# Thirty-two tokens of the second layer by gathered rows, modulation rows moved and halved, and wider gate products, in a two-layer backbone

## The chip, the cores and the metric

The kernel is one program on one core of a Trainium2 chip. Its time is the device time of one execution, in microseconds (us). A core has TensorE (PE: matrix products; the profile lists its weight loads apart as PEld), VectorE (DVE), ScalarE (ACT), GpSimd (POOL), SyncE (SP) and 16 DMA engines that all queues share. Each engine works through its own instructions in the order of the program.

## The reference

Two layers run over 256 context and 256 latent tokens of width 1024. In each, a modulated norm feeds four token mixers, and a second modulated norm `h` feeds a product-key expert layer. The modulation is six vectors (shift, scale and gate, twice), a product of silu(c) with a weight matrix: c for latents, c_ctx for context. Cut to the expert layer:

```python
def block(xb):                                  # 128 tokens
    qry = (xb @ wq).reshape(128, 8, 2, 128)
    s = einsum('thpk,hpnk->thpn', qry, sub_keys)
    sv, si = top_k(s, 16)                        # 16 of 128, for 8 heads x 2 halves
    cand_s = sv[:, :, 0, :, None] + sv[:, :, 1, None, :]
    cand_i = si[:, :, 0, :, None] * 128 + si[:, :, 1, None, :]
    fs, fpos = top_k(cand_s, 16)                 # 16 of the 256 pairs
    eidx = take_along_axis(cand_i, fpos)         # 8 x 16 = 128 experts of 16384
    gate = softmax(fs)
    act = gelu(einsum('td,thkd->thk', xb, u[eidx]))
    return einsum('thk,thkd->td', gate * act, v[eidx])
```

The second layer needs no context output: there the expert layer takes the 256 latents alone, and of its six vectors only the first two are used for both kinds of token.

## The kernel before

Tokens lie along the columns; the width lies on partitions in 8 blocks of 128 (`KD`). Products of high precision are three matmuls (`mm3`, L72 to L74): high x high, high x low, low x high, with each weight split by ACT (the high part) and DVE (what is left).

`peer(l)` is the expert layer, dense for most tokens: all 16384 experts are computed for all tokens and masked by gates. It has these stages.

- **Query stage** (`norm2`, `query`): 8 chunks of `wq`, then scores against the keys, then `top16` on DVE. After each chunk comes one pair of u-blocks.
- **u stage** (`u_blocks`): 64 pairs of blocks of 128 experts. A block takes 24 matmuls (8 x `mm3`) with `wd` columns, a gelu, and a store of the activation to DRAM (`ad`). `u_prep` loads a pair into one of 2 `raw` buffers and splits it into tiles of the pool `spl` (10 tiles). `wd` is 384 in layer 0 and 256 in layer 1.
- **Routing** (`route`, one per 128 tokens) turns the top 16 of each half into 128 expert numbers and gates per token (`fin`), all on DVE. It finds a key's index by comparing a position with 0..15 (L1295), multiplying by the indices (L1297) and adding up.
- **Gates** (`gate_hot`, `gates`): one-hot matrices per token, multiplied on PE into a 128x128 gate matrix (tile `pg`), 8 tokens a group, 16 groups per 128 tokens; stored to DRAM (`gd`), or, for the first 40 blocks of layer 1 (`FOLD`), multiplied at once into `kept`.
- **v stage** (`v_blocks`): again 64 pairs. Load v, activations (`va`) and gates (`vg`), multiply them (L1474), split the product into `wh` and `wl` and v into two `spl` tiles, and add 24 matmuls a block into 8 accumulators `f`.

In layer 0 the first 128 tokens are "apart": `tokens_apart` fetches for each the 128 rows of u that it needs, one gather of 128 rows of 4 KB a step (indirect DMA, issued by POOL), and multiplies each with `ht`, the token's own row of `h` (`dot`, L1384); the same for v, added into `facc` (L1391). That is 256 gathers. `rows_to` deals them out: `PHASE1` = 168 of them along the u stage, into tiles of `spl`, and the other 88 along the v stage, into 4 tiles `row`. Layer 1 has none.

`ada_row` computes 128 numbers of a modulation vector on DVE: a weight row tile (512 KB) times silu(c), summed along the row (L305), once for c and once for c_ctx. 56 of them run in layer 0's v stage, one after each pair: 8 for layer 0's last gate and all 48 of layer 1. `pin` keeps an instruction in the place of the program; otherwise a scheduler of the language chooses each engine's order when the program is built.

Of the kernel before, what the change touches and what calls it, by code (L numbers as in the profile page):

```python
# [12 lines left out]
U32 = mybir.dt.uint32  # L13
# [23 lines left out]
APART = 128  # L37
ROWS = 4
PHASE1 = 168
# [14 lines left out]
class Kernel:  # L54
# [39 lines left out]
    def build(self):  # L94
        tc, nc, A = self.tc, self.nc, self.A
        with ExitStack() as es:
# [25 lines left out]
            self.wd = [TA - APART, TC]  # L122
# [172 lines left out]
    def ada_row(self, pool, l, n):  # L295

        nc = self.nc
        if l not in self.mod:
            self.mod[l] = self.cst.tile([128, 6, KD, 2], F32, name=f"mod{l}")
        s, k = divmod(n, KD)  # L300
        w = pool.tile([128, 1024], F32, name="adaw", bufs=2)
# [4 lines left out]
        nc.vector.tensor_add(self.mod[l][:, s, k], self.mod[l][:, s, k], self.badat[:, l, s, k:k + 1].to_broadcast([128, 2]))  # L306
# [727 lines left out]
    def peer(self, l):  # L1034
# [5 lines left out]
        apart = (w - wd) // 128  # L1040
        with ExitStack() as es:
# [19 lines left out]
            with ExitStack() as e1:  # L1061
# [4 lines left out]
                with ExitStack() as e2:  # L1066
# [14 lines left out]
                    with self.order("DVE", "Activation"):  # L1081
# [6 lines left out]
                        self.norm2(aff, ts, hh, hl, self.rs_mm(w, scr, self.psum.tile([128, 512], F32, name="mm")), ht=ht)  # L1088
                    for ch in range(8):
# [5 lines left out]
                        u_pair()  # L1095
                sp = None
                if apart:
                    self.far = ep1(tc.tile_pool(name=f"far{l}", bufs=1, reuse_waits="tile"))
                with ExitStack() as e2:
# [12 lines left out]
                    if apart:  # L1112
# [3 lines left out]
                        sp = self.tokens_apart(l, fin[0], ht)  # L1116
                        next(sp)
                    first = apart
# [7 lines left out]
                    def u_next():  # L1126
                        u_pair()
                        rows_to(PHASE1 * (used[0] - u0) // (64 - u0))
                    for n, _ in enumerate(routes[first]):
                        if n % RN[l] == 0:  # L1130
                            u_next()
                    nd = nt - first
                    cost = [GW if t + 1 < nd else 1.0 for t in range(nd) for _ in range(16)]
                    left = 64 - used[0] - GL[l]
                    done = 0
                    sl = self.gate_slots(fin[first])
                    hot = self.gate_hot(sl, 0)
# [3 lines left out]
                    for x in range(16 * nd):  # L1141
                        t, g = divmod(x, 16)
                        while done < int(left * sum(cost[:x + 1]) / sum(cost) + 1e-6):
# [3 lines left out]
                        if t + 1 < nd:  # L1147
                            next(routes[first + t + 1], None)
                            if g == 14:
                                for _ in routes[first + t + 1]:  # L1150
                                    pass
                                sl2 = self.gate_slots(fin[first + t + 1])
# [617 lines left out]
```

## Time and profile before

| | |
|---|---|
| median of 3 runs | 2875.59 us (2870.84 to 2876.46) |
| profiled execution, its own time | 2874.08 us |
| its span, first to last instruction | 2872.0 us |
| busy: PE, DVE, ACT, POOL | 94%, 76%, 44%, 14% of the span |
| DMA | 662.88 MB, mean 231 GB/s |

A busy PE is not a PE at its peak: its matmuls overlap, so what one costs in a stream is the distance from start to start, not its duration. From the times of the matmuls, the stages lie as follows (us from the start): mixers of layer 0 to 427; query stage to 595; routing of the tokens apart to 655; rest of the u stage to 1202; v stage to 1775; mixers of layer 1 to 2029; query stage to 2135; routing and first gates to 2250; u stage to 2492; v stage to 2860.

### The profile page before, as it was taken

The page shows a single profiled execution, that of the slowest core. Times are in us where ns is not written, and L with a number is a line of the kernel's source. Part 1 is how long each engine was busy: PE and PEld are TensorE (multiplying, and loading weights), DVE is VectorE, ACT ScalarE, POOL GpSimd, SP SyncE. Part 2 cuts the span into 40 slices and gives each one's busy share as a digit, 9 for nine tenths or more (in the row PEclk, how much of TensorE's full clock was granted, in tenths as well). Part 3 has the DMA queues.
Part 4 walks back from the last instruction along what each step waited for, and adds up shares of the span by engine and source line. Part 5 has one row for each costly group of instructions (what it writes and reads, how often), then busy time and mean ns, then how long its engine had stood idle before and what let it go on. Part 6 is the DMA issues. An engine that isn't in the chain of part 4 may idle for free.

```text
span 2872.0 us, 47065 instructions
## 1 busy us (share of the span) xinstructions
PE 2701.9 (94%) x18199; PEld 2491.3 (87%) x18199; DVE 2178.1 (76%) x4703; ACT 1265.1 (44%) x2185; POOL 389.9 (14%) x354
## 2 busy tenths in 40 slices
PE   8989989999999987999999998988999999999998
PEld 5766758998888877999999997766999999999998
DVE  5665667689999976799999986655789767666665
ACT  5564644343344432343333334654545445444443
POOL 0010000004444343322222310000000000000000
PEclk9999899999999998999999999999999999999999
DMA  7111423237899999999999984211535766877774
GB/s 265 71 48 45 162 88 134 90 136 280 309 369 367 358 364 343 337 341 374 370 370 368 368 301 136 89 37 52 194 136 187 250 240 234 292 240 248 249 246 143
DMA packets 268752, 662.88 MB, mean 231 GB/s; under 512 B 16496, under 2 KB 146672, under 8 KB 258928
## 3 DMA queue, kind: packets, MB, share of 16 engines
q1 hardware_dynamic: 198688, 450.04, 45.0%
q0 software_dynamic: 36864, 134.23, 12.6%
q10 hardware_dynamic: 32976, 75.61, 6.9%
q8 instruction: 142, 2.33, 0.3%
q14 instruction: 82, 0.67, 0.1%
HBM read 585.37 MB, written 74.45 MB: 230 GB/s over the span
## 4 chain that ended last, share of the span: by engine, by line
PE 70%; DVE 16%; DMA 5%; issue 4%; ACT 3%; SPq 1%; POOL 0%; ACTq 0%; DVEq 0%; POOLq 0%
PE pu L72 8%; PE pu L74 8%; PE pu L73 8%; PE f L73 8%; PE f L74 8%; PE f L72 7%; PE fp L72 3%; PE fp L73 3%; PE fp L74 3%; PE pg L1349 2%; DVE junk L305 2%; DVE spl L1469 2%; PE mm L72 2%; PE mm L73 2%; PE mm L74 2%
## 5 line engine op out<-in xcount | busy, mean ns | idle before, releaser
L72 PE MATMUL pu<-h2h,spl 128*128 128x384 f32 (+1 forms) x2048 | 649.6, 317 | 39.4 <-ACT spl L1417 38.3
L73 PE MATMUL f<-wl,spl 128*128 128x384 f32 (+1 forms) x2048 | 635.3, 310 | 11.0 <-DVE wl L1476 11.0
L74 PE MATMUL pu<-h2h,spl 128*128 128x384 f32 (+1 forms) x2048 | 636.9, 313 | 8.2 <-DVE spl L1418 7.9
L73 PE MATMUL pu<-h2l,spl 128*128 128x384 f32 (+1 forms) x2048 | 639.4, 312 | 0.0
L74 PE MATMUL f<-wh,spl 128*128 128x384 f32 (+1 forms) x2048 | 629.2, 309 | 0.0
L72 PE MATMUL f<-wh,spl 128*128 128x384 f32 (+1 forms) x2048 | 511.7, 311 | 11.6 <-ACT wh L1475 8.4
L1468 ACT CAST spl<-raw 128x1024 fp32r<-128x1024 f32 x256 | 268.0, 1050 | 389.8 <-PE f L73 343.0
L72 PEld LDWEIGHTS pu<-h2h,spl 128*128 128x128 f32 x2048 | 393.0, 192 | 47.3 <-ACT spl L1417 44.0
L1469 DVE TENSOR_TENSOR spl<-raw,spl 128x1024 fp32r<-128x1024 f32 x256 | 312.6, 1225 | 158.8 <-ACT spl L1468 157.5
L1417 ACT CAST spl<-raw 128x1024 fp32r<-128x1024 f32 x256 | 266.6, 1049 | 343.1 <-PE pu L73 229.4
L73 PEld LDWEIGHTS f<-wl,spl 128*128 128x128 f32 x2048 | 389.7, 190 | 16.8 <-DVE wl L1476 16.1
L74 PEld LDWEIGHTS pu<-h2h,spl 128*128 128x128 f32 x2048 | 391.7, 191 | 12.7 <-DVE spl L1418 12.4
L1418 DVE TENSOR_TENSOR spl<-raw,spl 128x1024 fp32r<-128x1024 f32 x256 | 311.8, 1221 | 110.9 <-ACT spl L1417 108.8
L73 PEld LDWEIGHTS pu<-h2l,spl 128*128 128x128 f32 x2048 | 393.1, 192 | 0.3
L72 PEld LDWEIGHTS f<-wh,spl 128*128 128x128 f32 x2048 | 377.9, 190 | 16.1 <-ACT wh L1475 11.3
L74 PEld LDWEIGHTS f<-wh,spl 128*128 128x128 f32 x2048 | 389.2, 190 | 0.0
L418 DVE TENSOR_TENSOR spl<-raw,spl 128x512 fp32r<-128x512 f32 (+1 forms) x226 | 150.3, 704 | 72.7 <-ACT spl L414 62.5
L1435 ACT ACTIVATE act<-pu 128x384 f32<-128x384 f32 (+1 forms) x216 | 95.7, 443 | 218.7 <-PE pu L74 213.6
L1378 POOL DMA_INDIRECT spl<-in_un,ix x92 | 128.8, 1400 | 387.5 <-DVE fp L1246 244.0
L347 POOL TENSOR_TENSOR ms<-ms,mhalf 128x4 f32<-128x4 f32 (+1 forms) x5 | 4.8, 953 | 1264.1 <-DVE sq L345 833.9
L1475 ACT CAST wh<-va 128x384 fp32r<-128x384 f32 (+1 forms) x216 | 100.0, 467 | 168.5 <-PE f L74 79.5
L414 ACT CAST spl<-raw 128x512 fp32r<-128x512 f32 (+1 forms) x226 | 130.5, 629 | 76.8 <-PE fp L73 28.9
(305 smaller groups left out, 4547.6 us busy)
## 6 DMA issues: line engine op xcount, KB each, us to landing
raw<-in_ut SPq DMA_DIRECT2D x128, 1024.0 KB
raw<-in_v SPq DMA_DIRECT2D x128, 1024.0 KB
adaw<-in_wadat SPq DMA_DIRECT2D x56, 512.0 KB
ad<-act ACTq DMA_DIRECT2D x64, 384.0 KB
gd<-gstage ACTq DMA_DIRECT2D x12, 2048.0 KB
vg<-gd SPq DMA_DIRECT2D x32, 768.0 KB
va<-ad SPq DMA_DIRECT2D x64, 384.0 KB
raw<-in_win SPq DMA_DIRECT2D x22, 1024.0 KB
```

What stands on the lines that cost most here:

```text
L72: mm(ps, ah, bh, start=first, stop=False, **kw)
L73: mm(ps, ah, bl, start=False, stop=False, **kw)
L74: mm(ps, al, bh, start=False, stop=last, **kw)
L414: return self.nc.scalar.copy(p[0][o], w[:, o])
L418: return eng.tensor_tensor(p[1][o], w[:, o], p[0][o].bitcast(F32), op=ALU.subtract)
L1378: nc.gpsimd.indirect_dma_start(r, None, tabs[which], bass.IndirectOffsetOnAxis(ix[:, s:s + 1], 0))
L1417: self.pin(nc.scalar.copy(uh, self.u[:, n % 2]), n < 3)
L1418: self.pin(nc.vector.tensor_tensor(ul, self.u[:, n % 2], uh.bitcast(F32), op=ALU.subtract), n < 3)
L1435: nc.scalar.activation(a[:, b, :w], ps[:, :w], AF.Gelu)
L1468: nc.scalar.copy(vh, v[:, b])
L1469: nc.vector.tensor_tensor(vl, v[:, b], vh.bitcast(F32), op=ALU.subtract)
L1475: nc.scalar.copy(wh[:, :w], a[:, b, :w])
```

## The change

1. Layer 1 sets 32 of its 256 tokens apart (`APART = (128, 32)`), so that its u and v matmuls have 224 columns and 4 of its 32 gate groups fall away. A token's 128 experts are spread over four partitions: partitions q*32 to q*32+31 hold the same 32 tokens with 32 experts each, so there are 32 gathers of u rows and 32 of v rows. `ht` and `fin` are copied to the four quarters by small DMAs on SP, and a matrix `fsel` adds the quarters up at the end.
2. `PHASE1` is (144, 26): layer 0 makes 144 of its 256 gathers in the u stage and 112 in the v stage; layer 1 makes 26 of 64 in its u stage.
3. Of layer 1's modulation rows, those of the last four vectors are multiplied with silu(c) alone, not c_ctx. 24 of them move into layer 0's query stage, 4 after each chunk from the second on, with weight tile, junk tile and silu(c) in `spl`. The other 32 run after every other pair of the v stage, from one buffer `adaw` instead of two.
4. `v_blocks` multiplies and splits the gated values of both blocks of a pair in one instruction each.
5. `route` keeps the indices (`sif`) twice side by side, so that the multiplication's second operand has an innermost run of two.

```diff
-APART = 128
+APART = (128, 32)
-PHASE1 = 168
+PHASE1 = (144, 26)
...
-            self.wd = [TA - APART, TC]
+            self.wd = [TA - APART[0], TC - APART[1]]
...
-    def ada_row(self, pool, l, n):
+    def ada_row(self, w, junk, csb, l, n, nv):
...
-        for j in range(2):
+        for j in range(nv):
             o = self.mod[l][:, s, k, j:j + 1]
-            self.pin(nc.vector.scalar_tensor_tensor(self.junk, w, 1.0, self.csb[:, j], op0=ALU.mult, op1=ALU.mult, accum_out=o))
+            self.pin(nc.vector.scalar_tensor_tensor(junk, w, 1.0, csb[:, j], op0=ALU.mult, op1=ALU.mult, accum_out=o))
...
+                        for q in range(apart, 128, apart):
+                            nc.sync.dma_start(ht[q:q + apart], ht[0:apart])
+                    extra = list(range(16, 40)) if l == 0 else []
...
                         u_pair()
+                        if extra and ch == 0:
+                            csb = self.ada_vector()
+                        for _ in range(min(4, len(extra)) if ch else 0):
+                            w1, junk = (self.spl.tile([128, 1024], F32, name="spl") for _ in range(2))
+                            self.ada_row(w1, junk, csb, 1, extra.pop(0), 1)
...
-                        extra = [(0, n) for n in range(40, 48)] + [(1, n) for n in range(48)]
+                        extra = [(0, n, 2) for n in range(40, 48)] + [(1, n, 2) for n in range(16)] + [(1, n, 1) for n in range(40, 48)]
...
-                        if extra:
-                            self.ada_row(self.vp, *extra.pop(0))
+                        if extra and n % 2 == 0:
+                            self.ada_row(self.vp.tile([128, 1024], F32, name="adaw", bufs=1), self.junk, self.csb, *extra.pop(0))
...
-        sif = rw.tile([128, 8, 2, 16], BF16, name="sif")
-        nc.vector.tensor_copy(sif, si)
+        sif = rw.tile([128, 2, 128, 2], BF16, name="sif")
+        for j in range(2):
+            nc.vector.tensor_copy(sif[:, j].rearrange("p (h n) b -> p h n b", h=8), si[:, :, j, :, None].to_broadcast([128, 8, 16, 2]))
...
-            nc.vector.tensor_tensor(big, big, sif[:, :, j, :, None].to_broadcast(S4), op=ALU.mult)
+            bb = big.rearrange("p h n (a b) -> p (h n) a b", b=2)
+            nc.vector.tensor_tensor(bb, bb, sif[:, j, :, None].to_broadcast([128, 128, 8, 2]), op=ALU.mult)
...
+        S = n
+        if n < 128:
+            own = far.tile([128, 3, S], F32, name="own")
+            for q in range(128 // n):
+                nc.sync.dma_start(own[q * n:(q + 1) * n], fin[0:n, :, q * S:(q + 1) * S])
+            fin = own
...
+        wh, wl = (vp.tile([128, 2, w], F32R, name=x) for x in ("wh", "wl"))
+        if not fold:
+            av = a[:, :, :w].rearrange("p b (q t) -> p b q t", t=32)
+            nc.vector.tensor_mul(av, av, self.vg[:, :w // 32, i % 4:i % 4 + 2].rearrange("p q b t -> p b q t"))
+        nc.scalar.copy(wh, a[:, :, :w])
+        nc.vector.tensor_tensor(wl, a[:, :, :w], wh.bitcast(F32), op=ALU.subtract)
         for b in range(2):
             vh, vl = (self.spl.tile([128, 1024], F32R, name="spl") for _ in range(2))
...
-                    nc.tensor.transpose(acc[d][:, 0:128], self.facc[:, d * 128:(d + 1) * 128], self.ident)
+                    nc.tensor.matmul(acc[d][:, 0:off], self.facc[:, d * 128:(d + 1) * 128], self.fsel, start=True, stop=True)
```

The order of instructions, before and after, at three places follows. The changed kernel's lines have numbers of their own.

DVE in layer 0's query stage, around one chunk's end, before: the splits of `wq` (L418) and u (L1418), then the search for the largest scores (L1245).

```order
L1249 MAX_INDEX si_4115<-sv_4111,s 128x8 x2
L418 TENSOR_TENSOR spl<-raw,spl 128x512 x4
L1418 TENSOR_TENSOR spl<-raw,spl 128x1024
L1245 MAX sv_4108<-s 128x8 x2
L1245 MAX sv_4109<-s 128x8 x2
```

The same place after the change; L427 and L1449 are the splits, L1262 the search, L305 a modulation product and L306 its sum.

```order
L1266 MAX_INDEX si_4115<-sv_4111,s 128x8 x2
L1449 TENSOR_TENSOR spl<-raw,spl 128x1024
L306 TENSOR_TENSOR mod_4621<-mod_4621,badat 128x1
L1449 TENSOR_TENSOR spl<-raw,spl 128x1024
L427 TENSOR_TENSOR spl<-raw,spl 128x512 x2
L305 SCALAR_TENSOR_TENSOR spl,mod_4621<-spl 128x1024
L306 TENSOR_TENSOR mod_4621<-mod_4621,badat 128x1
L1262 MAX sv_4108<-s 128x8 x2
```

A modulation row, which waits for its weight tile, now stands between the splits that PE's next matmuls need and the search.

DVE in layer 0's v stage, before: products for the modulation (L305), the split of v (L1469), gating (L1474) and the split of the gated values (L1476), one block each, and the gathered rows (L1384, L1391).

```order
L1469 TENSOR_TENSOR spl<-raw,spl 128x1024
L305 SCALAR_TENSOR_TENSOR junk,mod_12303<-adaw,csb 128x1024 x2
L1469 TENSOR_TENSOR spl<-raw,spl 128x1024
L1474 TENSOR_TENSOR va<-va,vg 128x384
L306 TENSOR_TENSOR mod_12303<-mod_12303,badat 128x2
L1384 SCALAR_TENSOR_TENSOR junk,dots<-row,ht 128x1024
L1474 TENSOR_TENSOR va<-va,vg 128x384
L1391 SCALAR_TENSOR_TENSOR facc<-row,wt,facc 128x1024
L1476 TENSOR_TENSOR wl<-va,wh 128x384 x2
```

The same stage after: L1506 splits v, L1500 gates, L1502 splits the gated values, L1415 and L1422 use the gathered rows.

```order
L306 TENSOR_TENSOR mod_4621<-mod_4621,badat 128x2
L1415 SCALAR_TENSOR_TENSOR junk,dots<-row,ht 128x1024
L1422 SCALAR_TENSOR_TENSOR facc<-row,wt,facc 128x1024
L1415 SCALAR_TENSOR_TENSOR junk,dots<-row,ht 128x1024
L1422 SCALAR_TENSOR_TENSOR facc<-row,wt,facc 128x1024
L1500 TENSOR_TENSOR va<-va,vg 128x768
L1506 TENSOR_TENSOR spl<-raw,spl 128x1024 x2
L1502 TENSOR_TENSOR wl<-va,wh 128x768
L1506 TENSOR_TENSOR spl<-raw,spl 128x1024 x2
L305 SCALAR_TENSOR_TENSOR junk,mod_4621<-adaw,csb 128x1024
```

Two instructions of 768 columns stand where four of 384 stood, and more gathered rows stand between fewer modulation products.

SP's loads in layer 1 before: `wq` (L391) and u (L1415) up to the first v (L1457).

```order
L1415 DMA raw<-in_ut 128x2x1024 x4
L391 DMA raw<-in_wq 128x2048
L1415 DMA raw<-in_ut 128x2x1024
L391 DMA raw<-in_wq 128x2048
L1415 DMA raw<-in_ut 128x2x1024 x56
L1457 DMA raw<-in_v 128x2x1024 x2
```

After (L400, L1446 and L1488 are those loads; L1388 copies the routing result to the four quarters):

```order
L1446 DMA raw<-in_ut 128x2x1024 x4
L400 DMA raw<-in_wq 128x2048
L1446 DMA raw<-in_ut 128x2x1024
L400 DMA raw<-in_wq 128x2048
L1446 DMA raw<-in_ut 128x2x1024 x14
L1388 DMA own<-fin_18948 32x3x32 x4
L1446 DMA raw<-in_ut 128x2x1024 x42
L1488 DMA raw<-in_v 128x2x1024 x2
```

The copies wait for the routing of the first 128 tokens, and 42 loads of u are queued behind them.

## Rows read from the trace of the kernel before

**Rows 1.** The page: the span, and busy time of each engine.
```profile
span 2872.0 us, 47065 instructions
...
PE 2701.9 (94%) x18199; PEld 2491.3 (87%) x18199; DVE 2178.1 (76%) x4703; ACT 1265.1 (44%) x2185; POOL 389.9 (14%) x354
```
**Rows 2.** Busy time by stage: bounds, length, each engine's us (instructions), clock, DMA.
```profile
core 0: us, PE busy (x) PEld busy (x) DVE busy (x) ACT busy (x) POOL busy (x), PEclk, DMA share, GB/s
427.00:595.00 168.00, 166.83 (x877) 150.79 (x877) 114.08 (x515) 64.28 (x104) 0.00 (x0) 0.98 0.30 105
595.00:655.00 60.00, 60.00 (x348) 60.00 (x347) 60.00 (x325) 28.42 (x37) 0.00 (x0) 1.00 0.49 167
655.00:1202.00 547.00, 488.09 (x3145) 464.81 (x3143) 467.47 (x714) 198.65 (x308) 234.82 (x171) 0.96 0.93 345
1202.00:1695.00 493.00, 471.27 (x2666) 462.76 (x2667) 480.18 (x748) 174.78 (x233) 116.75 (x86) 1.00 1.00 360
2135.00:2250.00 115.00, 115.00 (x996) 114.47 (x996) 105.43 (x291) 60.41 (x95) 0.00 (x0) 1.00 0.59 202
2250.00:2492.00 242.00, 241.88 (x2216) 239.47 (x2215) 165.73 (x240) 118.78 (x207) 0.00 (x0) 1.00 0.71 248
2492.00:2860.00 368.00, 368.00 (x3064) 367.71 (x3062) 226.47 (x342) 170.85 (x255) 0.00 (x0) 1.00 0.70 235
```
**Rows 3.** Busy time by windows of 25 us, three of them, columns as in 2.
```profile
520.00:545.00 25.00, 25.00 (x131) 22.40 (x130) 17.73 (x90) 8.23 (x14) 0.00 (x0) 1.00 0.28 101
...
1370.00:1395.00 25.00, 25.00 (x145) 24.81 (x144) 24.93 (x38) 9.20 (x12) 6.54 (x5) 1.00 1.05 380
...
2145.00:2170.00 25.00, 25.00 (x209) 24.90 (x208) 25.00 (x134) 16.68 (x23) 0.00 (x0) 1.00 0.49 169
```
**Rows 4.** Timeline of PE, 384 columns: two matmuls with nine between them.
```profile
1199.18 0.34 PE L73 MATMUL pu<-h2l,spl 128*128 128x384 f32 x1
...
1200.91 0.34 PE L74 MATMUL pu<-h2h,spl 128*128 128x384 f32 x1
```
**Rows 5.** Busy time, 300 us of layer 1's v stage, 256 columns, columns as in 2.
```profile
2500.00:2800.00 300.00, 300.00 (x2502) 300.00 (x2502) 188.28 (x282) 141.81 (x209) 0.00 (x0) 1.00 0.74 249
```
**Rows 6.** Timeline of PE, score matmuls of 128 columns, 16 in a row.
```profile
445.99 1.95 PE L1236 MATMUL sk<-keys,s 128*128 128x128 f32 x16
```
**Rows 7.** Timeline of PE's weight loads right after them.
```profile
447.66 0.19 PEld L72 LDWEIGHTS mm<-h2h,spl 128*128 128x128 f32 x1
447.77 0.19 PEld L73 LDWEIGHTS mm<-h2l,spl 128*128 128x128 f32 x1
```
**Rows 8.** Groups by line and form: count, busy us, mean ns, idle before.
```profile
L1469 DVE TENSOR_TENSOR spl<-raw,spl 128x1024 fp32r<-128x1024 f32 x256 | 312.6, 1225 | 158.8 <-ACT spl L1468 157.5 <-PE f L74 0.8
...
L305 DVE SCALAR_TENSOR_TENSOR junk<-adaw,csb 128x1024 f32<-128x1024 f32 x112 | 137.0, 1224 | 0.4 <-DMA adaw<-in_wadat 0.2
...
L1384 DVE SCALAR_TENSOR_TENSOR junk<-spl,ht 128x1024 f32<-128x1024 f32 x92 | 112.4, 1222 | 9.1 <-DMA spl<-in_un,ix 9.0
...
L1349 PE MATMUL pg<-at,bt 128*128 128x128 f16 x1280 | 98.1, 224 | 10.6 <-DVE at L1335 9.2 <-issue 0.8 <-ACT gstage L1352 0.5
...
L1391 DVE SCALAR_TENSOR_TENSOR facc<-spl,wt,facc 128x1024 f32<-128x1024 f32 x75 | 96.2, 1282 | 0.4 <-DMA spl<-in_vn,ix 0.4
...
L1476 DVE TENSOR_TENSOR wl<-va,wh 128x384 fp32r<-128x384 f32 x128 | 69.9, 557 | 8.3 <-ACT wh L1475 8.0
...
L1297 DVE TENSOR_TENSOR big<-big,sif 128x2048 bf16<-128x2048 bf16 x12 | 27.5, 2291 | 0.0
...
L1295 DVE TENSOR_TENSOR big<-iob,posb 128x2048 bf16<-128x2048 bf16 x12 | 14.7, 1225 | 0.0
```
**Rows 9.** Waits from 655 to 1202: who waited for whom, us, times, longest.
```profile
POOL spl L1378 <- PE pu L74: 115.1, 31, 9.6
...
ACT spl L1417 <- DMA raw<-in_ut: 19.3, 5, 12.9
```
**Rows 10.** Waits from 427 to 655, columns as in 9.
```profile
ACT spl L1417 <- DMA raw<-in_ut: 4.6, 1, 4.6
```

More of the change, by code (lines that the diff above doesn't have):

```diff
@@ L1039, in peer @@
         wd = self.wd[l]
-        apart = (w - wd) // 128
+        apart = APART[l]
+        t0 = apart // 128
         with ExitStack() as es:
@@ L1115, in peer @@
                                 u_pair()
-                        sp = self.tokens_apart(l, fin[0], ht)
+                        sp = self.tokens_apart(l, fin[0], ht, apart)
                         next(sp)
-                    first = apart
                     u0, s0 = used[0], [0]
@@ L1127, in u_next @@
                         u_pair()
-                        rows_to(PHASE1 * (used[0] - u0) // (64 - u0))
-                    for n, _ in enumerate(routes[first]):
+                        rows_to(PHASE1[l] * (used[0] - u0) // (64 - u0))
+                    for n, _ in enumerate(routes[t0]):
                         if n % RN[l] == 0:
                             u_next()
-                    nd = nt - first
-                    cost = [GW if t + 1 < nd else 1.0 for t in range(nd) for _ in range(16)]
+                    todo = list(range(apart // 8, 16 * nt))
+                    cost = [GW if x // 16 + 1 < nt else 1.0 for x in todo]
                     left = 64 - used[0] - GL[l]
                     done = 0
-                    sl = self.gate_slots(fin[first])
-                    hot = self.gate_hot(sl, 0)
+                    sl = self.gate_slots(fin[t0])
+                    hot = self.gate_hot(sl, todo[0] % 16)
                     for _ in range(1 + l):
@@ L1140, in peer @@
                         done += 1
-                    for x in range(16 * nd):
+                    for n, x in enumerate(todo):
                         t, g = divmod(x, 16)
-                        while done < int(left * sum(cost[:x + 1]) / sum(cost) + 1e-6):
+                        while done < int(left * sum(cost[:n + 1]) / sum(cost) + 1e-6):
                             u_next()
@@ L1212, in norm2 @@
                 c = slice(k % 4 * 128, k % 4 * 128 + 128)
[L1213 removed]
+                nc.tensor.transpose(pt[0:na, c], t[:, 0:na], self.ident)
                 if k % 4 == 3:
[L1215 removed]
+                    nc.scalar.copy(ht[0:na, (k - 3) * 128:(k + 1) * 128], pt[0:na])
     def query(self, wsp, ch, hh, hl, w, keys, psk, sv, si):
@@ L1469, in v_blocks @@
             nc.vector.tensor_tensor(vl, v[:, b], vh.bitcast(F32), op=ALU.subtract)
[L1470 to L1477 removed]
+            parts.append((vh, vl, wh[:, b], wl[:, b]))
         def mm(d, b):
@@ L1491, in v_blocks @@
         full = ts.stop - ts.start
-        if off:
+        if l == 0:
             big = [vp.tile([128, 2, 1024], F32, name="csb", bufs=1).rearrange("p a b -> p (a b)")]
-            big += [vp.tile([128, 1024], F32, name="adaw", bufs=2) for _ in range(2)]
+            big += [vp.tile([128, 1024], F32, name="adaw", bufs=1), self.row_tile()]
             sqs = [t[:, a:a + 512] for t in big for a in range(0, t.shape[-1], 512)]
@@ L1749, in layout @@
     d["v"] = f["peer_v"].reshape(L, 128, 128, 1024)
-    d["un0"], d["vn0"] = (f[x][0].reshape(128, 128, 1024) for x in ("peer_u", "peer_v"))
+    for l in range(L):
+        for n in "uv":
+            d[f"{n}n{l}"] = f[f"peer_{n}"][l].reshape(128, 128, 1024)
     return d
```

76 lines of the change are left out of this document (39 added, 37 removed).

## The prediction

> **What bounds the kernel now.** The page comes first: PE is busy for 94% of 2872.0 us, DVE for 76% [rows 1]. Such shares are means over stages, so the table by stage is read next [rows 2], and it shows two different layers. In layer 1 PE is busy without a gap (241.88 of 242.00, 368.00 of 368.00) at clock 1.00, while DVE and the DMA engines stand near 65% and 70%: that layer is a stream of matmuls, and only cheaper or fewer matmuls shorten it. In layer 0 from 655 to 1695 PE idles 59 us of 547 and 22 us of 493, while the DMA share is 0.93 and 1.00 and DVE is busy 467 and 480 us. There DVE and DMA hold PE up together; the 25-us windows show both full at once (24.93 of 25 and 1.05, at 380 GB/s) [rows 3]. The waits name the link in the u stage: gathers wait 115.1 us for an `spl` tile that matmuls still read, and splits of u wait for loads up to 12.9 us [rows 9].
>
> The sum is made against the profiled execution's 2874.1 us, which is 1.5 us under the median of the runs shown.
>
> **Layer 0, query stage: +8 us.** 24 modulation rows come in, each a product of 1.224 us [rows 8] and a small sum that I put at 0.16 as an estimate (an eighth of the product), and one multiplication of 1.2 us: 34 us on DVE. From 427 to 595 DVE is idle 168 - 114 = 54 us [rows 2], about 7 us in each 25 [rows 3]. A chunk is 112 matmuls (48 of `wq`, 16 of scores, 48 of u) of the 131 in 25 us [rows 3], so 21.4 us, with 15.2 of DVE's work in it; four rows make it 20.7. So it fits, with nearly nothing to spare: behind a late row stand the split of u (PE) and the search (the routing, and so the first gather). The bounds are 0, all in idle time, and +34, none of it; I take 8, since 20.7 of 21.4 leaves no room for waits on four loads a chunk.
>
> **Layer 0, routing: -2 us.** The index multiplication costs 2.291 us, the comparison of the same shape beside it 1.225 [rows 8]. The new layout gives its second operand an innermost run, as the comparison's has, so I take 1.225; the bound is no gain. Two a routing, less one more copy of indices, save 1.8 us. This counts once, before the first gather, where DVE is busy 60.00 of 60.00 [rows 2]; later it lies beside other work.
>
> **Layer 0, u stage: -28 us.** 24 gathers leave it. Each costs DVE 1.222 or 1.282 us [rows 8], and the DMA 512 KB, 1.5 us at the stage's 345 GB/s [rows 2]: 30 us of DVE or 36 us of DMA, of a stage in which one or the other is full. PE's 59 idle us can absorb either. The bounds are 0 and -36; I take 28, somewhat less than both, because the two take turns.
>
> **Layer 0, v stage: -10 us.** DVE loses 56 of 112 products at 1.224: 68 us. Wider instructions: between 384 columns (557 ns) and 1024 (1225 ns) a column costs 1.04 ns [rows 8], so 768 cost 958 against 2 x 557, and 64 pairs with two such instructions save 20 us. 24 gathers come in: +30. Net -58 of 480 us. But the DMA, already at share 1.00, keeps its bytes: 24 gathers come, 24 weight tiles of the same 512 KB go. It moves 360 GB/s x 493 us = 177 MB, and at the best window's 380 GB/s that takes 467. The bounds are 0 (DMA is the limit) and -26; I take 10, nearer to none, since relief of DVE alone cannot speed a full queue.
>
> **Layer 1, narrower matmuls: -50 us.** Ten matmuls of 384 columns take 1.73 us, 173 ns each [rows 4]; 2502 of 256 columns take 300 us, 120 ns each [rows 5]. A column costs 0.415 ns, so 224 columns would cost 106.6 ns. No row shows so narrow a matmul of this kind. The nearest limit is the weight load: each matmul here loads 128 columns of weights, two loads without a full matmul between them stand 110 ns apart [rows 7], and 16 score matmuls of half the width, each with its load, take 1.95 us, the last one's own drain included, so no less than about 110 each [rows 6]. I take 111: 9 ns for each of 2 x 64 x 48 = 6144 matmuls, 55 us. From 2135 to 2250 DVE is busy 105 of 115 and at first 25.00 of 25 [rows 2, 3], so PE cannot run ahead there, and I give 5 back. The bounds are 0, if the pace stays at 120, and -82 at 106.6.
>
> The Trainium skill (TensorE: Matmul & The Clock Gate, "LDWEIGHTS (loading the stationary operand)") puts the load at the weights' columns over 1.2, 107 ns here, whatever the moving width. By that the saving would be 13 ns a matmul, 80 us before DVE's part; rows 7 show 110, and the sum goes by the rows.
>
> **Layer 1, the rest: +4 us.** Four gate groups fall away, 64 of 1280 gate matmuls that take 98.1 us [rows 8]: -5. DVE gets 32 x (1.222 + 1.282) = 80 us for 64 gathers. By 1.04 ns a column, two instructions of 256 columns cost 848 ns and one of 448 costs 624: the 64 splits and 44 gatings of its v stage save 24. So the three stages of rows 2 hold 498 + 56 us of DVE's work in some 680: 81%, off the limit, and that is the cover that hides the gathers. DMA: 26 gathers are 13.6 MB beside 248 GB/s x 242 us = 60 MB, 333 GB/s over 221 us; 38 are 20 MB beside 86 MB, 308 over 344. Both lie below the 360 that layer 0 sustains, but no longer far. In layer 0's u stage PE's idle time is 59 us for 168 gathers, 0.35 each; 64 of them would cost 22, and that is the upper bound. I take 9, because these stages start at share 0.70 and not 0.93. The copies on SP wait for routing that ends while u-pairs are still loaded ahead, so they are put at 0; if that cover goes, the 42 loads behind them slip by as much as routing is late.
>
> Sum: 8 - 2 - 28 - 10 - 50 + 4 = -78, so 2796 us by either base. All far bounds at once give 2874 - 2 - 36 - 26 - 82 - 5 = 2723 and 2874 + 34 + 22 = 2930.
>
> **The rivals.**
> A. The narrower matmul is no faster: 120 ns stay, because the 13.7 ns that the fit leaves at zero columns come on top of a load of some 107. For it: 256 columns alone are 106.2 by the fit, so that a load of that length plus the same 13.7 makes the same 120, and 256 may already be the floor. Against it: the score matmuls go 111. The term of -50 is then 0: 2846 us. The Trainium skill's rule above gives the load as 107, an estimate that fits this reading too.
> B. Layer 0 gives nothing: the DMA is the limit, and gathers taken from the u stage only let the next loads queue as before. For it: share 1.00 and 0.93. Against it: 12.6 MB really leave the stage for one that idles at 0.30. Then the sum is 8 - 2 - 50 + 4: 2834 us.
> C. It ends slower: each of the 24 rows of the query stage stands before DVE until its tile lands, and with DVE stand PE's splits. A load that was waited for in that stretch cost 4.6 us [rows 10]; 24 such waits are 110 us in place of 8: 2898 us. It decides from 3.6 us a row, (78 + 8) / 24. Against it: DMA share 0.30 there, and today's products, with two buffers, wait 0.2 us in all for theirs [rows 8].
> D. Better: 106.6 ns and DVE as layer 0's true limit: -82 + 5 in layer 1's matmuls and the far bounds in layer 0, 8 - 2 - 36 - 26 - 77 + 4: 2745 us.
>
> **How the numbers follow.** The forecast (2770 to 2822) gets 0.60, A 0.13, B 0.11, C 0.05, D 0.09, no change by mixtures 0.02. The range 2750 to 2846 takes in the forecast, B, most of D's upper part and A's middle, and leaves out less than 2 in 10. Within 0.2% (5.7 us, about what these runs spread) a measurement cannot tell from no change. Faster 0.93, same 0.02, slower 0.05.
>
> **What would show it.** Layer 1's v stage: the count of matmuls in 300 us rises from 2502 to about 2700 (111 ns), or stays (A). Layer 0: PE's idle time from 655 on falls from 81 to about 45 us and the u stage ends about 20 us earlier; the DMA share in the v stage stays near 1.00 while DVE's busy time falls by 55. Query stage: DVE busy near 148, and waits on the weight tiles under 10 us in all; over 80, C holds. In layer 1 DMA share rises to 0.9 with PE still without gaps. The forecast is wrong if gathers in layer 1 open gaps in PE, or if the routing of layer 0 ends over 20 us later than now.

## The result, and the profile after

| | before | after |
|---|---|---|
| median | 2876.03 us (2870.84 to 2879.08, 4 runs) | 2811.24 us (2804.03 to 2815.21, 4 runs) |
| profiled execution | 2874.08 us | 2815.21 us |
| span | 2872.0 us | 2813.4 us |

The ratio is 0.9774, with a 95% interval of 0.9749 to 0.9798: 65 us faster, where 78 were predicted. The profiled executions lie 59 us apart, and the tables below account for those 59. The time lies in the range, 15 us above the forecast. The terms of the sum came out quite otherwise, and that is what the experiments are about.

The page of the changed kernel, span and busy times [rows 1 before]:

```profile
span 2813.4 us, 46689 instructions
...
PE 2649.8 (94%) x18167; PEld 2446.7 (87%) x18167; DVE 2166.6 (77%) x4491; ACT 1244.3 (44%) x2059; POOL 478.8 (17%) x419
```

The shares hardly moved, so they say nothing on where the time went. The table by stage does: busy time of the changed kernel in the query stage, the routing, the u and v stages of layer 0, the routing, u and v stages of layer 1 (bounds, length, each engine's us and instructions, clock, DMA share, GB/s):

```profile
427.00:595.00 168.00, 167.51 (x878) 151.32 (x879) 144.21 (x590) 67.96 (x106) 0.00 (x0) 0.98 0.52 183
595.00:655.00 60.00, 60.00 (x348) 60.00 (x347) 60.00 (x333) 28.25 (x37) 0.00 (x0) 1.00 0.49 168
655.00:1171.00 516.00, 479.49 (x3144) 461.04 (x3143) 433.26 (x669) 198.63 (x306) 192.18 (x148) 0.97 0.93 343
1171.00:1650.00 479.00, 476.90 (x2741) 476.26 (x2740) 435.02 (x537) 174.00 (x184) 166.73 (x108) 1.00 1.01 369
...
2080.00:2190.00 110.00, 104.11 (x923) 103.28 (x923) 97.85 (x290) 55.90 (x87) 10.79 (x4) 0.97 0.59 201
...
2190.00:2428.00 238.00, 227.93 (x2199) 225.29 (x2197) 179.63 (x255) 115.68 (x203) 35.72 (x26) 1.00 0.83 291
2428.00:2802.00 374.00, 357.06 (x3098) 352.82 (x3098) 259.08 (x302) 159.95 (x201) 36.17 (x34) 0.99 0.82 284
```

Against [rows 2]: the query stage is as long as before although DVE has 30 us more in it. Layer 0's u stage ends at 1171 in place of 1202, and its v stage is now bound by PE (476.90 of 479), at the same full DMA. In layer 1 it is the other way round: PE stood at 241.88 of 242 and 368.00 of 368, and now idles 10 of 238 and 17 of 374, so stages with narrower matmuls are nearly as long as before. Idle time understates these stalls: a matmul of 224 columns lasts 0.27 us (in the timeline below) while the next is due after 0.11 us, so the first 0.16 us of a stall pass under a busy PE. The count shows the whole: from 2430 to 2730 the changed kernel starts 2486 matmuls, where the kernel before started 2502 in 300 us [rows 5] and the prediction asked for about 2700. From the start and end of the stages' matmuls:

| | before | after | change | predicted |
|---|---|---|---|---|
| query stage and routing (to the first gather) | 663.1 | 660.9 | -2 | +6 |
| layer 0, u stage from there | 537.8 | 509.8 | -28 | -28 |
| layer 0, v stage | 565.1 | 539.9 | -25 | -10 |
| layer 1, its mixers and first chunk | 280.6 | 284.0 | +3 | 0 |
| layer 1, u-pairs (first to last) | 441.5 | 437.1 | -4 | -46 with v |
| layer 1, v stage | 372.0 | 370.0 | -2 | |

Nearly the whole gain is layer 0's. The u-pairs and v stage of layer 1, where 46 us were expected, gave 6, and its mixers and first chunk took 3 more (not in `whole1`).

The waits in layer 1's v stage name what is late. Waits of the changed kernel from 2428 to 2802 (engine, line, what it waited for; us in all, times, longest):

```profile
ACT spl L1505 <- DMA raw<-in_v: 155.2, 50, 6.9
...
DVE spl L1506 <- ACT spl L1505: 44.4, 30, 5.5
DVE va L1500 <- DMA va<-ad: 32.8, 21, 4.2
...
PEld f L73 <- DVE wl L1502: 10.4, 13, 1.4
```

A stall of PE in the same kernel, from the timeline of SP's queue, POOL, DVE and PE (start, us, engine, line, operation; in brackets the idle time before and its end):

```profile
2591.81 0.37 SPq L1496 DMA_DIRECT2D va<-ad  x1
2592.95 0.37 SPq L1488 DMA_DIRECT2D raw<-in_v  x1
...
2594.33 0.94 POOL L1409 DMA_INDIRECT row<-in_un,ix  x1 [5.19 <-DVE junk L1415]
...
2596.28 0.62 DVE L1500 TENSOR_TENSOR va<-va,vg 128x448 f32<-128x448 f32 x1 [2.22 <-DMA va<-ad]
2596.82 1.22 DVE L1506 TENSOR_TENSOR spl<-raw,spl 128x1024 fp32r<-128x1024 f32 x1
2597.96 0.62 DVE L1502 TENSOR_TENSOR wl<-va,wh 128x448 fp32r<-128x448 f32 x1
...
2597.18 0.27 PE L72 MATMUL f<-wh,spl 128*128 128x224 f32 x1
2598.63 0.37 PE L73 MATMUL f<-wl,spl 128*128 128x224 f32 x1 [1.18 <-DVE wl L1502]
```

Read from the bottom: PE waits for `wl`, `wl` for its turn on DVE, and DVE had stood still for 2.22 us because 224 KB of activations, issued at 2591.81, came only at 2596.28, with a gather issued in between.

### The profile page after: what moved, and what is told of

Read it like the earlier page. It is cut to its first block, busy times and chain, and to the rows that moved or that the text cites. A ratio compares the mean times of both kernels' runs of the same rounds, so it can differ in the third digit from the quotient of the medians.

```text
span 2813.4 us, 46689 instructions
## 1 busy us (share of the span) xinstructions
PE 2649.8 (94%) x18167; PEld 2446.7 (87%) x18167; DVE 2166.6 (77%) x4491; ACT 1244.3 (44%) x2059; POOL 478.8 (17%) x419
## 5 line engine op out<-in xcount | busy, mean ns | idle before, releaser
L72 PE MATMUL pu<-h2h,spl 128*128 128x384 f32 (+1 forms) x2048 | 637.3, 311 | 40.7 <-ACT spl L1448 27.7
L73 PE MATMUL f<-wl,spl 128*128 128x384 f32 (+1 forms) x2048 | 623.9, 306 | 8.0 <-DVE wl L1502 8.0
L74 PE MATMUL pu<-h2h,spl 128*128 128x384 f32 (+1 forms) x2048 | 628.9, 308 | 2.6 <-DVE spl L1449 2.6
L73 PE MATMUL pu<-h2l,spl 128*128 128x384 f32 (+1 forms) x2048 | 629.5, 307 | 0.0
L74 PE MATMUL f<-wh,spl 128*128 128x384 f32 (+1 forms) x2048 | 609.7, 305 | 2.3 <-DVE spl L1506 2.3
L72 PE MATMUL f<-wh,spl 128*128 128x384 f32 (+1 forms) x2048 | 568.4, 307 | 8.8 <-ACT act L1466 4.6
L1506 DVE TENSOR_TENSOR spl<-raw,spl 128x1024 fp32r<-128x1024 f32 x256 | 308.4, 1219 | 93.4 <-ACT spl L1505 85.1
L1449 DVE TENSOR_TENSOR spl<-raw,spl 128x1024 fp32r<-128x1024 f32 x256 | 310.3, 1218 | 47.9 <-ACT spl L1448 38.3
L427 DVE TENSOR_TENSOR spl<-raw,spl 128x512 fp32r<-128x512 f32 (+1 forms) x226 | 149.4, 699 | 65.4 <-ACT spl L423 56.3
L1409 POOL DMA_INDIRECT row<-in_vn,ix x87 | 125.4, 1441 | 374.6 <-DVE facc L1422 316.3
L1501 ACT CAST wh<-va 128x768 fp32r<-128x768 f32 (+1 forms) x108 | 78.3, 725 | 231.3 <-DVE va L1500 131.6
L72 PE MATMUL fp<-s,spl 128*128 128x512 f32 (+1 forms) x416 | 161.2, 387 | 2.1 <-DVE s L666 1.2
```

Of the source, the lines that this page charges most:

```text
L72: mm(ps, ah, bh, start=first, stop=False, **kw)
L73: mm(ps, ah, bl, start=False, stop=False, **kw)
L74: mm(ps, al, bh, start=False, stop=last, **kw)
L427: return eng.tensor_tensor(p[1][o], w[:, o], p[0][o].bitcast(F32), op=ALU.subtract)
L1409: nc.gpsimd.indirect_dma_start(r, None, tabs[which], bass.IndirectOffsetOnAxis(ix[:, s:s + 1], 0))
L1449: self.pin(nc.vector.tensor_tensor(ul, self.u[:, n % 2], uh.bitcast(F32), op=ALU.subtract), n < 3)
```

## The experiments

Each time is given as a ratio to the kernel before on the same chip; 0.001 is 2.9 us, and the changed kernel stands at 0.9774.

**Is it the gathers, and what of them?** `nogather1` drops the work of layer 1's 32 tokens:

```diff
+        if l:
+            nc.vector.memset(self.facc, 0.0)
+            return
         yield
         for c in range(0, S + C, C):
...
```

> Layer 1 still computes 224 columns, but neither gathers the rows of its 32 tokens nor multiplies them (their part of its output is left out). In the changed kernel layer 1's u and v stages hold 60 us of TensorE stalls where the kernel before held 13. Three theories of these 47 us. Load theory: the 64 gathers of 512 KB delay the loads of u and v, which have two buffers; without gathers the stalls go back to about 13 us, so 2811 - 47 = 2764 us. VectorE theory: the gathers' 64 instructions of 1.2 to 1.3 us stand ahead of the splits; here they are gone too, so also 2764. Pace theory: a pair of blocks now takes 5.4 us of TensorE, less than a load of 1 MB, its split and its release take in turn, whatever else runs; the stalls stay and the time is 2800 to 2811. This run tells the third from the first two.

Measured: 2768.17 us, 0.9631 (0.9603 to 0.9660). The pace theory falls.

`nodma1` keeps DVE's instructions and drops the transfers:

```diff
         def gather(which, s):
+            if l:
+                return ht
             r = self.row_tile()
```

> Layer 1's 64 instructions on VectorE stay, but they read a tile that is already there, and the 64 gathers are not issued (the values of the 32 tokens are wrong). Load theory: the stalls go, 2764 us, as without gathers. VectorE theory: they stay, 2811. Pace theory: 2800 to 2811.

Measured: 2766.34 us, 0.9612 (0.9582 to 0.9643): all of it comes back without the transfers.

`nodve1` keeps the transfers and cuts DVE's part:

```diff
             r = gather(0, s)
+            if l:
+                nc.vector.scalar_tensor_tensor(junk[:, :8], r[:, :8], 1.0, ht[:, :8], op0=ALU.mult, op1=ALU.mult, accum_out=dots[:, s:s + 1])
+                return
...
```

> Layer 1's 64 gathers stay, but of each gathered row VectorE reads only 8 elements, so its 1.2 to 1.3 us fall to about 0.1 (the values of the 32 tokens are wrong). Load theory: the stalls stay, 2811 us. VectorE theory: they go, 2764. If both count, both this run and the one without transfers lie between, and their gains add to about 47.

Measured: 2818.05 us, 0.9791 (0.9758 to 0.9824): nothing comes back. So it is the transfers, in three runs that agree. Busy time of `nodve1` in its v stage shows where: DVE lets the row tiles go at once, so the 34 gathers run together in the first 112 us.

```profile
2428.00:2540.00 112.00, 97.33 (x731) 96.05 (x731) 56.05 (x113) 37.11 (x50) 40.56 (x34) 0.86 1.00 368
2540.00:2802.00 262.00, 260.40 (x2332) 260.22 (x2331) 156.93 (x181) 118.57 (x144) 0.00 (x0) 1.00 0.73 242
```

While they run the DMA moves as much as in layer 0's v stage (1.00, 368 GB/s), PE idles 15 us, and its granted clock is 0.86, so that part of the time it stands at the lower of its two levels (1.2 for 2.4 GHz), which costs up to another 0.14 x 112 = 16 us; together they are about the 30 us by which 731 matmuls at 111.6 ns (82 us) fall short of 112. After the gathers PE idles 1.6 us in 262. The Trainium skill (DMA: Bandwidth & Descriptors, "Queues, rings and completion order") says that a DMA engine takes turns between its queues packet by packet. By that a gather in one queue would lengthen a load in another; these windows agree, though no run shows the packets' order.

The same view of `nodma1`, u stage, v stage and 300 us of the latter:

```profile
2190.00:2408.00 218.00, 218.00 (x2102) 216.69 (x2101) 174.32 (x246) 111.43 (x198) 0.00 (x0) 1.00 0.74 256
2408.00:2755.00 347.00, 346.47 (x3095) 345.73 (x3093) 253.54 (x297) 158.47 (x198) 0.00 (x0) 1.00 0.74 243
2430.00:2730.00 300.00, 300.00 (x2689) 300.00 (x2688) 220.40 (x253) 137.91 (x168) 0.00 (x0) 1.00 0.76 250
```

2689 matmuls in 300 us are 111.6 ns each, against 119.9 in [rows 5]. DVE's work alone opens no gap.

In the u stage this run also leaves free the `spl` tiles that the gathers hold there, so that the tiles are a rival to the bytes; `half1`, below, keeps the tiles.

**Is the treatment of 32 tokens worth anything?** `whole1` leaves layer 1 whole and keeps the rest of the change:

```diff
-APART = (128, 32)
+APART = (128, 0)
...
```

> Layer 1 treats no token apart (256 columns, no gathers, its own gates), all else as in the changed kernel. Layer 0 should then show its whole gain by itself. By the traces layer 0 ended 57 us earlier, so 2876 - 57 = 2819 us if the two-blocks-at-a-time gating costs layer 1 nothing, and the whole treatment of 32 tokens apart was worth only 8 us. By the sum of my prediction layer 0 gives 32: 2844. If the joint gating of two blocks itself stalls layer 1, the time is above 2819 by that and the v stage of layer 1 shows idle TensorE at 256 columns, where the kernel before had 1.5 us.

Measured: 2813.83 us, 0.9781 (0.9752 to 0.9809), like the changed kernel. So layer 0 gives the whole gain, and in layer 1 the gathers' cost eats what the narrower matmuls bring. Joint gating by itself opens no gap there (PE 371.34 of 372.00 in its v stage).

**Bytes, or number?**

```diff
+        H = slice(0, 512 if l else 1024)
...
-            nc.gpsimd.indirect_dma_start(r, None, tabs[which], ...)
+            nc.gpsimd.indirect_dma_start(r[:, H], None, tabs[which], ...)
...
```

> The 64 gathers of layer 1 fetch rows of 512 values in place of 1024, as many rows as before, and VectorE multiplies 512 (the 32 tokens' values are wrong). The run without transfers was 46 us faster than the changed kernel. If the cost goes by bytes, half of it goes: 2811 - 23 = 2788. If it is a cost of each gather or each row, it stays: 2805 to 2811. If it is a delay that two buffers cover up to some length, more than half goes: 2770 to 2780.

Measured: 2786.68 us, 0.9709 (0.9680 to 0.9738): 19 us back by the ratios, of the 47 that all transfers cost, give or take 11. That fits bytes (23) and excludes a cost that stays with the number of gathers; some more or less than half can't be told apart. VectorE's part is halved too, but `nodve1` showed that it brings nothing. By the traces the u-pairs take 428 us (changed kernel 437, `nodma1` 415) and the v stage 360 (370, 348): about half of the loss comes back in either. In the v stage the gathers have tiles of their own, and in the u stage `half1` holds as many `spl` tiles as the changed kernel, so the tiles can be no more than a part there.

**Depth, or capacity?** A third buffer for layer 1's loads needs room, so twelve more blocks go through memory, which `fold14` does alone:

```diff
-FOLD, QS, VA = (0, 20), (10, 6), (2, 3)
+FOLD, QS, VA = (0, 14), (10, 6), (2, 3)
```

> A control for the next run, which needs room: layer 1 keeps 28 of its 128 blocks of activations on the chip in place of 40, and twelve more go through memory and back. By the load theory these are 12 x 114 KB written and 12 x 229 KB read beside some 240 MB of a layer, so 0 to +8 us: 2811 to 2819.

Measured: 2802.93 us, 0.9757 (0.9740 to 0.9774). No cost is seen: layer 1's u-pairs and v stage take 808 us as against 807. The profiled run is ahead in layer 0 (u stage to 1163), where this edit changes nothing; the other kernels on its chip are ahead there too (below).

`raw3` adds the buffer:

```diff
+            self.rx = ep(tc.tile_pool(name="rx", bufs=1, reuse_waits="tile")) if l else self.raw
...
-            self.u = self.raw.tile([128, 2048], ...)
+            self.u = (self.rx if n % 6 == 4 else self.raw).tile([128, 2048], ...)
...
-        v = self.raw.tile([128, 2048], ...)
+        v = (self.rx if n % 3 == 2 else self.raw).tile([128, 2048], ...)
```

> As the control, with a third buffer for the loads of u and v in layer 1. The runs before showed that the transfers of the 64 gathers cost layer 1 some 45 us. Two forms of that. Depth theory: the bytes fit (DMA share 0.82), but a load that shares the engines with a gather lands some 2 us later, and two buffers don't cover this at 5.4 us a pair; a third buffer does, so the stalls go, and the time is that of the control less 40 to 45, about 2770. Capacity theory: in the stretches with gathers the DMA engines are full, and every byte costs; a third buffer changes less than 10 us, so 2805 to 2815.

Measured: 2776.50 us, 0.9664 (0.9648 to 0.9680): 27 us less than the control, give or take 7, where the depth theory had 40 to 45 and the capacity theory less than 10. Busy time of `raw3`, u and v stage of layer 1:

```profile
2190.00:2411.00 221.00, 217.18 (x2106) 215.95 (x2103) 169.04 (x244) 113.03 (x196) 37.38 (x26) 1.00 0.87 312
2411.00:2766.00 355.00, 351.51 (x3094) 350.84 (x3094) 262.84 (x308) 162.54 (x199) 49.55 (x34) 0.99 0.87 300
```

The same bytes go at a higher rate, and PE idles 4 and 3.5 us. So depth is the larger part; what is left over the run without transfers (0.9664 against 0.9612, some 15 us) was not taken further. The waits of four kernels in layer 1's v stage show how two buffers came to be too few. ACT's split of v waits, in `whole1`:

```profile
ACT spl L1505 <- PE f L73: 157.3, 104, 1.9
...
ACT spl L1505 <- DMA raw<-in_v: 24.8, 11, 4.6
```

in `nodma1`:

```profile
ACT spl L1507 <- DMA raw<-in_v: 135.4, 49, 5.0
...
ACT spl L1507 <- PE f L73: 17.4, 15, 3.6
```

and in `raw3`:

```profile
ACT spl L1506 <- PE f L73: 102.7, 76, 2.2
```

At 256 columns the split waits for PE to free a tile: the load is early. At 224 columns, even with no gather, it waits for the load 49 times, yet PE has no gap: the loop of load, split and release just keeps up with it. The changed kernel's 155.2 us look like 20 more on this wait; by this reading its slack had gone before, and what a gather adds falls to PE. With a third buffer the split waits for PE again. No run has the gathers at 256 columns, so that they would cost less there is read from these waits and not tried.

**What made layer 0's v stage shorter?** `vsingle` undoes the joint gating (the old loop of one block, as in the diff of the change):

```diff
-        nc.scalar.copy(wh, a[:, :, :w])
-        nc.vector.tensor_tensor(wl, a[:, :, :w], wh.bitcast(F32), op=ALU.subtract)
...
+            nc.scalar.copy(wh[:, :w], a[:, b, :w])
+            nc.vector.tensor_tensor(wl[:, :w], a[:, b, :w], wh[:, :w].bitcast(F32), op=ALU.subtract)
```

> The v stages gate and split their activations one block at a time again, as in the kernel before, all else as in the changed kernel. In the prediction the joint form saves VectorE 20 us in layer 0 and 24 in layer 1. VectorE-limit theory (layer 0's v stage went from 566 to 540 us because VectorE was its limit): VectorE is busy 435 of 479 us there now, 455 with this, so TensorE stays the limit and little comes back, 0 to +10: 2811 to 2821. Rival: the joint form is itself what costs layer 1 its stalls, since both blocks' activations must be there before the first split; then the v stage of layer 1 gets up to 20 us shorter: 2791 to 2800.

Measured: 2811.92 us, 0.9789 (0.9759 to 0.9818), as the changed kernel within the interval. The stages tell more. `fold14` ran on the same chip and has the same layer 0: its u stage ends at 1163 and its v stage takes 539 us; here they are 1160 and 556.5, so the v stage is 17 longer (as against the changed kernel). Layer 1 is no worse for the joint form: its v stage takes as long as in the changed kernel, so the rival falls. In layer 0 PE waits again for the gated values, as in the kernel before. Busy time of `vsingle` in that stage, then its waits from 1205 to 1650:

```profile
1171.00:1650.00 479.00, 466.54 (x2649) 457.86 (x2648) 432.52 (x633) 176.36 (x233) 172.21 (x108) 1.00 1.00 363
...
PEld f L73 <- DVE wl L1507: 11.2, 19, 1.2
...
PEld f L72 <- ACT wh L1506: 6.3, 5, 2.1
```

The waits of the kernel before in the same window:

```profile
PEld f L73 <- DVE wl L1476: 13.5, 15, 2.9
...
PEld f L72 <- ACT wh L1475: 8.8, 7, 2.7
```

The changed kernel has neither wait there. So 17.5 of the 22 us of these waits, and 17 of the 25 us by which the stage got shorter, come back with single gating alone. DVE is busy 432 of 479 us in `vsingle`, less than in the changed kernel, and moves as many bytes: these waits need no full DVE, only gated values that come late.

`prod2` makes the stage's products twice:

```diff
-            self.pin(nc.vector.scalar_tensor_tensor(junk, w, 1.0, csb[:, j], ...))
+            for _ in range(1 + (junk is getattr(self, "junk", None))):
+                self.pin(nc.vector.scalar_tensor_tensor(junk, w, 1.0, csb[:, j], ...))
```

> Every modulation product of layer 0's v stage is made twice (56 instructions of 1.22 us more on VectorE, 112 in all as in the kernel before; the bytes moved and the result are unchanged). VectorE-limit theory: VectorE needs 435 + 68 = 503 us in a stretch that holds 479, so the v stage gets at least 24 us longer: 2835 to 2845. DMA theory, on which the prediction's small v term rested: the queue is as full as before, VectorE only waits less, and the time stays at 2811 to 2817.

Measured: 2839.39 us, 0.9881 (0.9864 to 0.9897), 31 us more than the changed kernel by the ratios, with the same bytes. Busy time of `prod2` in the v stage up to 1650, and late in it:

```profile
1162.00:1650.00 488.00, 481.76 (x2764) 480.11 (x2763) 470.48 (x608) 173.08 (x184) 146.47 (x92) 1.00 0.97 344
...
1550.00:1650.00 100.00, 100.00 (x579) 100.00 (x578) 97.01 (x129) 33.10 (x35) 31.05 (x20) 1.00 1.00 351
1650.00:1735.00 85.00, 62.66 (x333) 59.53 (x331) 71.26 (x96) 19.81 (x24) 22.00 (x16) 0.86 0.69 252
```

DVE is nearly full (470 of 488 us), yet up to 1650 PE keeps almost the changed kernel's pace: 2764 matmuls in 488 us, 177 ns each, against 2741 in 479, 175. DVE falls behind with the gathered rows instead, and 16 gathers are left for the end, where PE waits (the changed kernel has none after 1650): eight rows stand behind DVE's last split of v, and PE's first product with `facc` waits 12 us for them. So DVE's work sets the length of the stage at unchanged bytes, but the two runs show it in two places: with single gating PE loses time all along the stage, as the kernel before did, and with twice the products it loses it at the end. What halving the products brings beside single gating, as the kernel before had it, no run shows by itself; 8 of the 25 us are left for it, net of the 24 gathers that the stage holds more than before.

`adav` takes the 24 rows back into the v stage:

```diff
-                    extra = list(range(16, 40)) if l == 0 else []
+                    extra = []
...
-                        if extra and n % 2 == 0:
+                        if extra and (n % 2 == 0 or n < 48):
```

> The 24 modulation rows of the query stage go back to layer 0's v stage (one product each, as now), all else as in the changed kernel. The prediction put them at +8 us in the query stage; the trace of the changed kernel shows that stage no longer than before. If they are free there, taking them away saves 0 to 2 us there. In the v stage they bring 24 x 1.4 = 34 us of VectorE and 24 x 512 KB. If VectorE alone was the limit of that stage, it goes to 469 of 479 us and the time rises by 0 to 15: 2811 to 2826. If the DMA limits too (share 1.01 at 369 GB/s), 12.6 MB are 34 us more: 2845.

Measured: 2901.27 us, 1.0104 (1.0087 to 1.0121): 95 us more than the changed kernel by the ratios, beyond either figure. Busy time of `adav` in the v stage, and near its end:

```profile
1161.00:1550.00 389.00, 386.90 (x2221) 386.26 (x2221) 333.09 (x420) 142.97 (x151) 91.57 (x57) 1.00 0.95 338
1700.00:1750.00 50.00, 0.00 (x0) 0.00 (x0) 32.83 (x51) 0.22 (x1) 24.31 (x19) 0.50 0.82 276
```

By 1550 only 57 gathers are out (84 in the changed kernel), and the rest run at the end with PE at 0.00. Neither DVE (333 of 389) nor the DMA (0.95) was full: the order decides. In DVE's order 219 of the 256 gathered rows stand ahead of the last split of v, against all 256 in the changed kernel; the 37 rows behind it are covered by nothing, and PE's first product with `facc` waits 83 us for them. So this run doesn't price a row as meant; it says that the stage has no place for 24 more rows in this order.

**The u stage.** `phase168` has `PHASE1 = (168, 26)` in place of `(144, 26)`.

> 168 of layer 0's 256 gathers stand in its u stage again, as in the kernel before, and 88 in its v stage; all else as in the changed kernel. The prediction's u term: 24 gathers cost the u stage 28 us, so its end goes from 1171 back to about 1199. The v stage is bound by TensorE now (476.9 of 479 us busy), so 24 gathers fewer give it nothing back: 2811 + 28 = 2839. Rival: the u stage got shorter because the gathers' loads compete less by other means (the routing, the query stage), or the stall only changes its place: 2811 to 2817.

Measured: 2823.11 us, 0.9846 (0.9814 to 0.9877): 21 us more by the ratios, give or take 11, so the u term holds, at a little under its 28. The stage ends at 1182 here. In the changed kernel and the runs that leave this stage as it is, it ends anywhere from 1160 to 1173, and most of that goes with the chip: 1167 to 1173 in the four runs on the first, 1160 to 1164 in the four on the second, 1161 and 1162 in the two on the chip of `phase168`. Against those two it ends 20 us later, about what the ratios say. Whether the 24 gathers held the stage by DVE or by the DMA was not tried.

**A better version.** `best` is `raw3` with 32 modulation rows in the query stage and 136 gathers in the u stage:

```diff
-PHASE1 = (144, 26)
+PHASE1 = (136, 26)
...
-                    extra = list(range(16, 40)) if l == 0 else []
+                    extra = list(range(16, 48)) if l == 0 else []
...
-                        for _ in range(min(4, len(extra)) if ch else 0):
+                        for _ in range(min(5, len(extra)) if ch else 0):
...
```

> The version with three buffers for layer 1's loads, and the change taken one step further in layer 0: 32 modulation rows in the query stage in place of 24 (up to five a chunk), 24 in the v stage, and 136 gathers in the u stage in place of 144. By the u term, eight gathers fewer are worth 9 to 10 us there; the v stage keeps its bytes; the query stage has VectorE busy 144 of 168 us and gets 11 more. If these still find idle time: 2776 - 9 = 2767. If the query stage is full with them, the rows come back as up to 11 us: 2776 to 2780.

Measured: 2775.15 us, 0.9666 (0.9650 to 0.9682), no different from `raw3`. Busy time of its query stage:

```profile
427.00:595.00 168.00, 167.98 (x881) 151.80 (x882) 150.67 (x610) 65.53 (x104) 0.00 (x0) 0.99 0.56 199
```

PE doesn't feel the eight more rows, but the first gather does. From the first matmul of the query stage to the first gather the kernel before takes 234.8 us, `best` 237.4, and every other kernel with the change 233.1 to 233.3, `adav` with no row there too. So 24 rows cost nothing, and eight more cost 4 us. From that gather the u stage takes 495 us against 500 in `half1` and `prod2` on the same chip: eight gathers fewer bring 5 us where 9 were put, and the two cancel. Of both, `raw3` has the smaller edit, and it is 1.1% faster than the changed kernel.

## Why the prediction came out near, point by point

The total was off by only 15 us because errors of opposite sign nearly cancel: layer 1 came 40 us short of its sum, while layer 0's v stage brought 15 more than put, and the query stage with the routing 8 more. That the time lies in the range is luck: by the prediction's own sign of being wrong, gathers that open gaps in PE, its account of layer 1 is wrong.

- **Query stage, +8: too dear.** The first gather comes 2 us earlier, not 6 later, and `adav`, without the rows, is no faster to it (233.2 us from the first matmul of the query stage, as with them). The rows waited for their tiles little, as the waits of the changed kernel from 427 to 595 show, under the 10 us named, and PE kept going. Rival C is refuted.

```profile
ACT spl L1448 <- DVE spl L305: 14.8, 9, 2.3
...
DVE spl L305 <- DMA spl<-in_wadat: 9.0, 5, 3.2
```

- **Routing, -2: right.** `adav` has no rows in the query stage and still comes to its first gather 1.5 us sooner than the kernel before (233.2 against 234.8); of the change, only the new routing is left there. The index multiplication takes 1.218 us, where 1.225 was put.
- **Layer 0, u stage, -28: about right** (-28 between the profiles; 21, give or take 11, with the gathers put back). Rival B is refuted.
- **Layer 0, v stage, -10: mis-sized, -25.** The step that failed is "relief of DVE alone cannot speed a full queue". The queue's share of 1.00 at 360 GB/s was no ceiling: 369 were reached, and PE waited for DVE. `vsingle` and `prod2` show it without a change in bytes: the single gating makes the stage 17 us longer, twice the products 31, the one by late gated values and the other by rows left over at the end. So the two don't add to the 25.
- **Layer 1, narrower matmuls, -50: right.** 111.6 ns where 111 was put; `nodma1` takes 763 us for u-pairs and v stage, 50 less than before, the gate groups' 5 included. Rival A is refuted. The rule of the Trainium skill that was weighed (TensorE: Matmul & The Clock Gate, "LDWEIGHTS (loading the stationary operand)") gives 107 ns; the rows stay 4 to 5 above it. The 5 us "given back" while DVE is full are 2 at most: `nodma1` has PE busy 110.15 of 112.00 us in the routing, with DVE at 106.76. The changed kernel's 6 idle us there (104.11 of 110) come with its first gathers, for whose rows DVE waits 8.2 us.
- **Layer 1, the rest, +4: the step that failed most.** 64 gathers cost 44 us (807 against 763), 0.69 each, where 9 were put and 22 was the bound. I took the price from layer 0's idle time per gather and scaled it down by the DMA share. But a share is a mean: what counted was whether a load that shares the engines with a gather still lands within the time of its pair. By narrowing the matmul the same edit shortened that time from 2 x 24 x 120 = 5.8 to 5.4 us and, by the waits of `whole1` and `nodma1`, used up the slack that I had read in the kernel before; the two halves of the edit were priced apart. The bound itself came from a stage with 2 x 24 x 173 = 8.3 us a pair, and from idle PE alone: by that measure the changed kernel's layer 1 loses 27 us, 0.42 a gather, close to the bound's 0.35, while the stages lose 44. The prediction had the dearer price beside it, 28 / 24 = 1.2 us for a gather in layer 0's u stage. The sign of error that the prediction named, gathers that open gaps in PE, is what the trace shows.
- **The copies on SP, 0: right.** `nodma1` keeps them, and in its u stage PE is busy 218.00 of 218.00 us.

Rival D had layer 0's v stage about right and the matmul wrong.

## What to carry to other kernels

When an edit makes the bounding engine faster, price everything else in that stage against the new, shorter period: a mean share of 0.70 says nothing on whether a double-buffered load still arrives in time. Read the wait ahead of the load's first user: while it waits for a buffer to be freed by the bounding engine there is slack, and once it waits for the transfer, further bytes cost (in `half1` about half the loss for half the bytes). Before paying for such an edit in transfers, look whether one more buffer restores the slack. And measure the loss by matmuls started in a stretch, not by idle time alone.

## What the runs showed of the hardware

- 224-column matmuls, each with its own 128-column weight load, go at 111.6 ns (2689 in 300 us), while 256 columns take 119.9 (2503 in 300 us in `whole1`). A fit through 256 and 384 columns would give 106.6, so the line already bends here.
- The 16 DMA engines held 369 to 371 GB/s over 479 us of layer 0's v stage (changed kernel and `whole1`, share 1.01 and 1.02), against 360 in the kernel before at 1.00: a share of 1.00 did not mean that no more could be moved.
- A 512 KB gather cost PE 0.69 us where the load loop had no slack left, 0.25 with a third buffer (16 us for 64, by `raw3` against `nodma1` in the same stages: 779 against 763), and 0.87 in layer 0's u stage (21 us for 24, give or take 11).
